# Unit products of a float32 matmul kernel: the low-part products written between the high-part products

## The chip, the cores and the metric

The kernel runs on one core of a Trainium2 chip. The metric is the device time of one execution in microseconds (us). Five engines work side by side, each through its own queue in order: TensorE (PE, its weight loads shown apart as PEld), VectorE (DVE), ScalarE (ACT), GpSimd (POOL) and SyncE (SP), which issues most of the transfers.

## What is computed

One block of a hybrid encoder trunk on 256 tokens of width 2048, all in float32. The parts of the reference that matter here:

```
u = RMSNorm_pre(x)                                # x: 256 x 2048
proj = u @ w_in                                   # q/k/v of two attentions, RWKV inputs, gates
y_a, y_b = stick_breaking(...), forgetting(...)   # 4 heads x 128 each
y_c = rwkv7_time_mix(...)                         # 16 heads x 64, chunks of 64
m = g_a*(y_a @ w_branch_a) + g_b*(y_b @ w_branch_b) + g_c*(y_c @ w_branch_c)
x = x + RMSNorm_post(m @ w_out)
hdn = square(relu(RMSNorm_pre2(x) @ w_mlp_up))    # 2048 -> 8192
x = x + RMSNorm_post2(hdn @ w_mlp_down)           # 8192 -> 2048
```

## The kernel before, in words

Every large product is made in three parts. An operand is split into a high part (rounded by ScalarE to the format `float32r` that TensorE takes) and a low part (what VectorE finds left over): `wsplit` (lines 150 to 160) does so for each weight tile of 128 x 1024 that SyncE brings in (`wraw`, line 145), in line 158 on ScalarE (`whi`) and line 159 on VectorE (`wlo`). Then high times high, high times low and low times high are summed; low times low is left out.

An activation tile `pk` is 128 x 512: 256 columns of the high part and beside them 256 of the low part. So a product of a high weight block with the whole `pk` gives two of the three sums at once, over 512 columns (called a high product here); a product of the low weight block with the first half of `pk` gives the third, over 256 columns (a low product). A weight block of 128 x 128 is loaded into TensorE for each product.

There are two forms of large product. In `tok` (lines 195 to 232; its products stand in lines 204 and 220) the activations are the loaded side and the weights the moving one, so all its products have 512 columns; it makes values, gates, branches and output projections. In `gemm` (line 170) the weights are the loaded side. `gemm` takes one half of a unit: 8 weight blocks (`hi`, `lo`) against 8 activation tiles. `unit` (line 184) calls it twice for one output tile of 128 features, the second time with `last` set. It serves 40 units of the projection (queries, keys, the low-rank inputs, the RWKV inputs). The up-projection of the MLP (`up`, line 1342) calls `gemm` itself for 62 more output tiles, in two halves that stand apart in a list of work with the products of the down-projection (lines 1478 to 1480, all of 512 columns) in between. That makes 204 calls with 16 products each: 1632 high ones (lines 174 and 182) and 1632 low ones (line 178).

Before the change, `gemm` writes all high products first (line 174), then all low ones (line 178). In the second half of a unit the last high product is kept back and closes the sum, behind the low ones (line 182).

TensorE's order is the order in which the program is written, up to the end of the first stage; the other engines' queues are ordered by the framework's scheduler. The attentions and the RWKV recurrence ("mixers") run as threads beside the units: `tick` moves a clock of the program forward by the estimated time of the products just written (`US` = 0.227 us for 512 columns), and a thread whose due time has come writes its next step at that place, so its small products stand inside a unit. A thread says with `yield 3.0` how long its next step has to wait. `gemm` ticks after every second high product and after every fourth low one: 12 `US` in a first half, 10 in a second one. `up` calls `gemm` without a clock.

`sb_mix` (line 428 on) is one such thread. Its chain runs ScalarE (lines 437, 443, 445), VectorE (441, 442, 452, 453), eight masking products on GpSimd (line 456), ScalarE again (line 462, the split) and VectorE (line 463). ScalarE's queue also holds `whi` (line 158) for the units, so what waits there holds up the weights.

Weight tiles of the split kind have three buffers each (`whi`, `wlo`); the split of the next half is written before the products of the present one.

Of the kernel before, what the change touches and what calls it, by code (L numbers as in the profile page):

```python
# [22 lines left out]
US = 0.227  # L23
# [27 lines left out]
def hybrid_block(ctx, tc, xt, x, gains, params, consts, lora, gup, wst, out):  # L51
    nc = tc.nc
    V, A, G, PE = nc.vector, nc.scalar, nc.gpsimd, nc.tensor
# [52 lines left out]
    def step(th):  # L106

        if th["need"] is not None:
            if th["need"] not in at or clock[0] < at[th["need"]] + SETTLE:
                return False  # L110
            th["need"] = None
        if clock[0] < th["due"]:
            return False
        try:
            r = next(th["gen"])
        except StopIteration:
            threads.remove(th)
            return True
        if isinstance(r, str):
            th["need"] = r  # L120
        else:
            th["due"] = clock[0] + r
        return True

    def tick(us):

        clock[0] += us
        while any([step(th) for th in list(threads)]):
            pass
# [40 lines left out]
    def gemm(ps, hi, lo, pks, first, last, tick=lambda us: None):  # L170

        n = len(pks)
        for i in range(n - 1 if last else n):
            PE.matmul(ps, hi[:, i * 128:i * 128 + 128], pks[i], start=first and i == 0, stop=False)  # L174
            if i % 2:
                tick(2 * US)
        for i in range(n):
            PE.matmul(ps[:, 0:T], lo[:, i * 128:i * 128 + 128], pks[i][:, 0:T], start=False, stop=False)  # L178
            if i % 4 == 3:
                tick(2 * US)  # L180
        if last:
            PE.matmul(ps, hi[:, (n - 1) * 128:n * 128], pks[n - 1], start=False, stop=True)  # L182

    def unit(pks):

        ps = gps()
        for h in range(2):
            hi, lo = wnext()
            gemm(ps, hi, lo, pks[8 * h:8 * h + 8], h == 0, h == 1, tick)
        return ps  # L190
# [221 lines left out]
    for h in range(8):  # L412
        ps = qb[h] if h < 3 else unit(upk)
# [641 lines left out]
    for s in ("q", "k"):  # L1055
        lst = []
        for h in range(4):
            ps = unit(upk)
# [12 lines left out]
    for hf in range(2):  # L1071
        for s, mo in (("k", MU_K), ("r", MU_R), ("v", MU_V)):
            for p in range(4 * hf, 4 * hf + 4):
                ps = unit(upk)
# [278 lines left out]
    def up(j):  # L1353
# [3 lines left out]
        def run(hl, half):  # L1357
            if half == 0:
                ps[0] = gps()
            gemm(ps[0], hl[0], hl[1], upk2[8 * half:8 * half + 8], half == 0, half == 1)  # L1360
            if half:
                urgent.append(post)
# [163 lines left out]
    for j in range(2):  # L1526
        up(j)
        ps, post = heads[j]
# [23 lines left out]
    for b in range(4):  # L1552
        for sb in range(2):
            for d, F in enumerate(down(b, sb)):
# [3 lines left out]
                last = b == 3 and sb == 1 and d == SIZES[3] // 4 - 1  # L1558
# [211 lines left out]
```

## Time and profile before

| | |
|---|---|
| runs of the kernel before | 1493.69, 1495.75, 1497.37 us (median 1495.75) |
| span of the profiled execution | 1493.8 us; the page gives no other time for it |
| DVE busy in the span | 1213.1 us (81%) |
| ACT busy in the span | 933.9 us (63%) |
| moved by DMA | 317.70 MB, mean 213 GB/s |

The page of the profile lists the busy time of each engine, the span in 40 slices, the chain of work that ended last, and groups of instructions by line. A row of a group reads: line, engine, operation, output<-inputs, shapes, count | busy time, mean time of one in ns | idle time of the engine before them and who ended it. A row of the timeline reads: start in us, length in us, engine, line, operation, tiles, shapes, count of equal instructions in a row, and in brackets the engine's idle time before it. Products of TensorE overlap, so the length of one is longer than its share of the time: what a product costs is read from the distance between starts.

### The profile page before, as it was taken

How to read it: one execution, taken by the hardware profiler on the slowest of the kernel's cores; microseconds unless marked ns; L12 is line 12 of the kernel's file. 1: busy time of each engine (PE TensorE's matmuls, PEld its weight loads, DVE VectorE, ACT ScalarE, POOL GpSimd, SP SyncE). 2: the span in 40 equal slices, each digit the busy share in tenths (PEclk: the TensorE clock that was granted, in tenths of full speed). 3: DMA queues.
4: the chain of work that ended last, by engine and by line, in shares of the span. 5: the costliest groups of instructions: out<-in, count | busy, mean ns of one | idle time of the engine just before them, and what ended most of it. 6: DMA issues, size and time to landing. Idle time of an engine off the chain costs nothing.

```text
span 1493.8 us, 22852 instructions
## 1 busy us (share of the span) xinstructions
PE 1480.8 (99%) x8427; PEld 1250.7 (84%) x8427; DVE 1213.1 (81%) x1688; ACT 933.9 (63%) x1396; POOL 91.3 (6%) x160
## 2 busy tenths in 40 slices
PE   9999999999999999999999999999999999999997
PEld 8888888888778888788888888888888888888885
DVE  7666677999679798567547788999899999999996
ACT  7465666664576554474444777776766776777663
POOL 0021000100001100000000000000000000000000
PEclk9999999999999999999999999999999999999999
DMA  7545455545544545445755868888888788889874
GB/s 282 188 148 191 163 170 180 172 162 198 171 153 161 184 169 209 144 151 194 269 196 204 275 213 249 255 257 259 242 232 264 238 262 248 260 248 283 259 250 151
DMA packets 107759, 317.70 MB, mean 213 GB/s; under 512 B 10752, under 2 KB 14976, under 8 KB 107392
## 3 DMA queue, kind: packets, MB, share of 16 engines
q1 hardware_dynamic: 94688, 284.39, 54.9%
q0 software_dynamic: 8064, 29.36, 10.5%
q10 hardware_dynamic: 4896, 2.49, 0.6%
q8 instruction: 66, 1.08, 0.3%
q14 instruction: 45, 0.37, 0.1%
HBM read 282.65 MB, written 4.19 MB: 192 GB/s over the span
## 4 chain that ended last, share of the span: by engine, by line
PE 96%; DVE 1%; ACT 1%; issue 1%; POOL 0%; POOLq 0%; DVEq 0%; ACTq 0%
PE gps L220 28%; PE gps L174 23%; PE gps L178 13%; PE gps L204 7%; PE mps L1478 3%; PE mps L1479 3%; PE mps L1480 3%; PE gps L1480 3%; PE gps L1478 2%; PE gps L1479 2%; PE gps L182 2%; PE gps L340 1%; PE mps L791 1%; PE mps L281 0%; PE gps L1237 0%
## 5 line engine op out<-in xcount | busy, mean ns | idle before, releaser
L159 DVE TENSOR_TENSOR wlo<-raw,whi 128x1024 fp32r<-128x1024 f32 x497 | 602.7, 1220 | 157.2 <-ACT whi L158 140.7
L158 ACT ACTIVATE whi<-raw 128x1024 fp32r<-128x1024 f32 x497 | 522.0, 1056 | 249.7 <-PE gps L220 101.1
L174 PE MATMUL gps<-pk,whi 128*128 128x512 f32 x1336 | 336.5, 391 | 0.4 <-ACT whi L158 0.4
L174 PEld LDWEIGHTS gps<-pk,whi 128*128 128x128 f32 x1336 | 247.3, 188 | 48.8 <-ACT whi L158 0.6
L220 PE MATMUL gps<-whi,pk 128*128 128x512 f32 x1136 | 286.0, 391 | 0.0
L220 PEld LDWEIGHTS gps<-whi,pk 128*128 128x128 f32 x1136 | 211.5, 188 | 44.0
L178 PEld LDWEIGHTS gps<-pk,wlo 128*128 128x128 f32 x1424 | 194.1, 190 | 14.1 <-DVE wlo L159 0.3
L178 PE MATMUL gps<-pk,wlo 128*128 128x256 f32 x1424 | 199.3, 282 | 0.0
L220 PE MATMUL gps<-wlo,pk 128*128 128x512 f32 x568 | 155.3, 392 | 0.0
L220 PEld LDWEIGHTS gps<-wlo,pk 128*128 128x128 f32 x568 | 105.7, 188 | 21.9
L1341 DVE TENSOR_TENSOR sp<-raw,sp 128x1024 fp32r<-128x1024 f32 x67 | 81.7, 1220 | 6.7 <-ACT sp L1340 6.5
L1340 ACT ACTIVATE sp<-raw 128x1024 fp32r<-128x1024 f32 x67 | 70.6, 1054 | 19.6 <-DMA raw<-in_wst_dram 6.3
L1369 ACT ACTIVATE sp<-gps 128x512 f32<-128x512 f32 x52 | 31.1, 598 | 72.1 <-PE gps L182 72.1
L204 PE MATMUL gps<-whi,pk 128*128 128x512 f32 x256 | 68.9, 390 | 0.0
L1478 PE MATMUL mps<-whi,fm 128*128 128x512 f32 x168 | 66.1, 394 | 0.0
L1479 PE MATMUL mps<-whi,fm 128*128 128x512 f32 x168 | 65.8, 392 | 0.0
L1480 PE MATMUL mps<-wlo,fm 128*128 128x512 f32 x168 | 65.5, 390 | 0.0
L1440 POOL DMA_DIRECT2D raw<-raw x40 | 34.9, 873 | 431.1 <-DVE raw L1437 111.7
L204 PEld LDWEIGHTS gps<-whi,pk 128*128 128x128 f32 x256 | 47.8, 188 | 9.9
L1480 PE MATMUL gps<-wlo,fm 128*128 128x512 f32 x126 | 49.4, 392 | 0.5 <-DVE wlo L159 0.4
L1478 PE MATMUL gps<-whi,fm 128*128 128x512 f32 x126 | 49.2, 391 | 0.0
L1437 DVE TENSOR_TENSOR raw<-raw,raw 128x1024 f32<-128x1024 f32 x40 | 48.8, 1220 | 0.4
(393 smaller groups left out, 2009.1 us busy)
## 6 DMA issues: line engine op xcount, KB each, us to landing
raw<-in_wst_dram SPq DMA_DIRECT2D x499, 512.0 KB, 4.4
raw<-raw POOLq DMA_DIRECT2D x40, 512.0 KB, 7.6
sp<-in_wst_dram SPq DMA_DIRECT2D x16, 512.0 KB, 5.4
raw<-sp POOLq DMA_DIRECT2D x8, 512.0 KB, 6.9
sp<-raw POOLq DMA_DIRECT2D x8, 512.0 KB, 7.0
x<-in_x_dram SPq DMA_DIRECT2D x8, 256.0 KB, 5.5
xs<-x SPq DMA_DIRECT2D x2, 1024.0 KB, 4.9
x<-xs SPq DMA_DIRECT2D x4, 512.0 KB, 6.2
```

What stands on the lines that cost most here:

```text
L158: A.activation(hi, raw, AF.Copy)
L159: V.tensor_tensor(lo, raw, hi.bitcast(F32), ALU.subtract)
L174: PE.matmul(ps, hi[:, i * 128:i * 128 + 128], pks[i], start=first and i == 0, stop=False)
L178: PE.matmul(ps[:, 0:T], lo[:, i * 128:i * 128 + 128], pks[i][:, 0:T], start=False, stop=False)
L204: PE.matmul(ps[tt], pks[k][:, c:c + 128], w[:, (k - k0) * 512:(k - k0) * 512 + 512], start=k == 0 and part == 0 and w is hl[0], stop=w is ...
L220: PE.matmul(ps[tt], pks[k][:, c:c + 128], w[:, (k - k0) * 512:(k - k0) * 512 + 512], start=k == 0 and part == 0 and w is hl[0], stop=False)
L1340: A.activation(hi, raw, AF.Copy)
L1341: V.tensor_tensor(lo, raw, hi.bitcast(F32), ALU.subtract)
L1437: V.tensor_tensor(x, x, z, ALU.add)
L1478: PE.matmul(Q[f], p, w, start=d == 0 and i == 0, stop=False)
L1479: PE.matmul(Q[f], pl, w, start=False, stop=False)
L1480: PE.matmul(Q[f], p, wl, start=False, stop=d == nd - 1 and i == 1)
```

## The change

Only `gemm` is changed. It writes three high products, then a low and a high one in turn until the high ones are used up, then the low ones that are left. In a second half the closing high product is still the last, and one more low product comes ahead of it. The clock is moved by the whole time of the products: 12 `US` in a first half as before, and 12 instead of 10 in a second half.

```diff
-        for i in range(n - 1 if last else n):
-            PE.matmul(ps, hi[:, i * 128:i * 128 + 128], pks[i], start=first and i == 0, stop=False)
-            if i % 2:
-                tick(2 * US)
-        for i in range(n):
+        lag = 3
+        end = n - 1 if last else n
+
+        def high(i):
+            PE.matmul(ps, hi[:, i * 128:i * 128 + 128], pks[i], start=first and i == 0, stop=last and i == n - 1)
+
+        def low(i):
             PE.matmul(ps[:, 0:T], lo[:, i * 128:i * 128 + 128], pks[i][:, 0:T], start=False, stop=False)
-            if i % 4 == 3:
-                tick(2 * US)
+
+        for i in range(lag):
+            high(i)
+        tick(lag * US)
+        for i in range(n - (1 if last else 0)):
+            low(i)
+            if i + lag < end:
+                high(i + lag)
+                tick(1.5 * US)
+            else:
+                tick(0.5 * US)
         if last:
-            PE.matmul(ps, hi[:, (n - 1) * 128:n * 128], pks[n - 1], start=False, stop=True)
+            low(n - 1)
+            high(n - 1)
+            tick(1.5 * US)
```

In the changed kernel the high products stand in line 177, the low ones in line 180, and every later line is 13 further down (158 and 159 stay; 437 becomes 450, 445 becomes 458, 456 becomes 469, 462 becomes 475).

TensorE's queue, second half of the unit `gps_964` in the first stage (`pk` are the activation tiles, `whi` and `wlo` the weight parts). Before:

```order
L174 MATMUL gps_964<-pk_222,whi_967 128x512
L174 MATMUL gps_964<-pk_225,whi_967 128x512
L174 MATMUL gps_964<-pk_228,whi_967 128x512
L174 MATMUL gps_964<-pk_231,whi_967 128x512
L174 MATMUL gps_964<-pk_244,whi_967 128x512
L174 MATMUL gps_964<-pk_247,whi_967 128x512
L174 MATMUL gps_964<-pk_250,whi_967 128x512
L178 MATMUL gps_964<-pk_222,wlo_968 128x256
L178 MATMUL gps_964<-pk_225,wlo_968 128x256
L178 MATMUL gps_964<-pk_228,wlo_968 128x256
```

The same half now:

```order
L177 MATMUL gps_970<-pk_222,whi_973 128x512
L177 MATMUL gps_970<-pk_225,whi_973 128x512
L177 MATMUL gps_970<-pk_228,whi_973 128x512
L180 MATMUL gps_970<-pk_222,wlo_974 128x256
L177 MATMUL gps_970<-pk_231,whi_973 128x512
L180 MATMUL gps_970<-pk_225,wlo_974 128x256
L177 MATMUL gps_970<-pk_244,whi_973 128x512
L180 MATMUL gps_970<-pk_228,wlo_974 128x256
L177 MATMUL gps_970<-pk_247,whi_973 128x512
L180 MATMUL gps_970<-pk_231,wlo_974 128x256
L177 MATMUL gps_970<-pk_250,whi_973 128x512
L180 MATMUL gps_970<-pk_244,wlo_974 128x256
```

The first low product, which reads the VectorE tile `wlo`, moves from behind seven high products to behind three; four low products in a row remain at the end, of which the last is cut off here.

ScalarE's queue while `sb_mix` runs beside the units (`sbt` and `sbh` are tiles of that thread, `zp` and `zz` of the low-rank inputs, `raw` a weight tile as it came). Before:

```order
L443 ACTIVATE sbt<-sbt 128x768 x2
L593 ACTIVATE tmp_842<-gps_774 36x256
L158 ACTIVATE whi_876<-raw_874 128x1024
L445 ACT_TABLE_LOAD
L445 ACTIVATE sbt<-sbt 128x1536
L596 ACTIVATE zp_844<-tmp_843,par 36x256
L158 ACTIVATE whi_907<-raw_905 128x1024
L610 ACT_TABLE_LOAD
L610 ACTIVATE zz<-zz 32x256
L233 ACTIVATE tmp_900<-gps_851 128x256
L158 ACTIVATE whi_939<-raw_937 128x1024
L462 ACTIVATE sbh<-sbt 128x768
```

The same stretch now:

```order
L456 ACTIVATE sbt<-sbt 128x768
L606 ACTIVATE tmp_842<-gps_774 36x256
L158 ACTIVATE whi_879<-raw_877 128x1024
L456 ACTIVATE sbt<-sbt 128x768
L609 ACTIVATE zp_844<-tmp_843,par 36x256
L458 ACT_TABLE_LOAD
L458 ACTIVATE sbt<-sbt 128x1536
L158 ACTIVATE whi_917<-raw_915 128x1024
L623 ACT_TABLE_LOAD
L623 ACTIVATE zz<-zz 32x256
L246 ACTIVATE tmp_910<-gps_851 128x256
L158 ACTIVATE whi_939<-raw_937 128x1024
```

One of the two exponentials (line 443, now 456) and the scaling of the low-rank input (line 596, now 609) have moved to between the weight split and the table load ahead of the logarithm (line 445, now 458).

VectorE's queue for the same chain, where the two operations that follow the logarithm stand (lines 452 and 453, now 465 and 466). Before:

```order
L452 TENSOR_TENSOR sbt<-sbm,sbt 128x768
L597 SCALAR_TENSOR_TENSOR zz<-tmp_843,omu,zp_844 36x256
L453 TENSOR_TENSOR sbt<-sbt 128x768
L159 TENSOR_TENSOR wlo_908<-raw_905,whi_907 128x1024
L452 TENSOR_TENSOR sbt<-sbm,sbt 128x768
```

Now:

```order
L610 SCALAR_TENSOR_TENSOR zz<-tmp_843,omu,zp_844 36x256
L465 TENSOR_TENSOR sbt<-sbm,sbt 128x768 x2
L466 TENSOR_TENSOR sbt<-sbt 128x768
L159 TENSOR_TENSOR wlo_918<-raw_915,whi_917 128x1024
L247 TENSOR_TENSOR g_146_909<-gps_851,tmp_910 128x256
```

Both halves of the first operation now stand ahead of the first half of the second, which GpSimd waits for.

## Prediction, made before the changed kernel was run

> **What bounds the kernel now.** I read the page first: engines, slices, waits of TensorE.
>
> ```profile
> span 1493.8 us, 22852 instructions
> ...
> PE 1480.8 (99%) x8427; PEld 1250.7 (84%) x8427; DVE 1213.1 (81%) x1688; ACT 933.9 (63%) x1396; POOL 91.3 (6%) x160
> ...
> L178 PE MATMUL gps<-pk,wlo 128*128 128x256 f32 x1424 | 199.3, 282 | 0.0
> ```
>
> ```profile
> PE gps L174 <- ACT whi L158: 0.4, 1, 0.4
> ```
>
> TensorE is busy for 1480.8 of 1493.8 us, and the second row, from the list of its waits, is the only wait of line 174: 0.4 us in one place. So the time is set by the pace at which TensorE takes products, and by no other engine. The change adds and removes no product; it can only alter that pace, or bring new waits.
>
> The pace is the distance between starts. The chain that ended last has a long run of nothing but high products (`tok`), and the timeline of TensorE has one unit alone:
>
> ```profile
> 54.28 19.06 PE gps L220 x84
> ```
>
> ```profile
> 24.57 2.00 PE L174 MATMUL gps<-pk,whi 128*128 128x512 f32 x8
> 26.41 1.12 PE L178 MATMUL gps<-pk,wlo 128*128 128x256 f32 x8
> 27.36 1.78 PE L174 MATMUL gps<-pk,whi 128*128 128x512 f32 x7
> 28.98 1.11 PE L178 MATMUL gps<-pk,wlo 128*128 128x256 f32 x8
> 29.93 0.40 PE L182 MATMUL gps<-pk,whi 128*128 128x512 f32 x1
> 30.16 2.00 PE L174 MATMUL gps<-pk,whi 128*128 128x512 f32 x8
> ```
>
> A settled high product costs 19.06/84 = 0.227 us. The unit from 24.57 to 30.16 costs 5.59 us for 16 pairs of a high and a low product: 0.3494 a pair. Its first eight low ones take 27.36 - 26.41 = 0.95, or 0.119 each. But its first eight high ones take 1.84, or 0.230 each: behind low products the high ones are slower than in a long run. A 256-column product at half the price of a 512-column one would cost 0.1135. So there is a reserve: if all went at 0.227 and 0.1135, a pair would cost 0.3405, 0.009 less than now, and 1632 pairs 14.5 us less. The question is how much of it the new order can reach.
>
> **The pace of products in turn.** No stretch of this trace alternates as the new order does, but there are places with one high product between low ones, and a few that show the extremes (timeline of TensorE; the first rows are small products of the mixers with the same shapes):
>
> ```profile
> 116.78 0.28 PE L472 MATMUL mps<-sbh,tri 128*128 128x256 f32 x1
> 116.90 0.28 PE L472 MATMUL mps<-sbl,tri 128*128 128x256 f32 x1
> 117.01 0.39 PE L479 MATMUL mps<-sbh,tri 128*128 128x512 f32 x1
> 117.24 0.40 PE L481 MATMUL mps<-sbl,tri 128*128 128x256 f32 x2
> 117.47 1.08 PE L174 MATMUL gps<-pk,whi 128*128 128x512 f32 x4
> ...
> 457.64 0.39 PE L220 MATMUL gps<-wlo,pk 128*128 128x512 f32 x1
> 457.87 0.28 PE L1004 MATMUL mps<-syh,gup 128*128 128x256 f32 x1
> 457.98 0.28 PE L1004 MATMUL mps<-syl,gup 128*128 128x256 f32 x1
> 458.10 0.28 PE L1004 MATMUL mps<-syh,gup 128*128 128x256 f32 x1
> 458.22 0.27 PE L1004 MATMUL mps<-z,gup 128*128 128x256 f32 x1
> ...
> 825.89 0.40 PE L1237 MATMUL gps<-pk,w 128*128 128x512 f32 x1
> 826.13 0.39 PE L1237 MATMUL gps<-pk,whi 128*128 128x512 f32 x1
> ```
>
> A low product right behind a high one costs 0.11 (457.87 to 457.98), a later one of the run 0.12 (457.98 to 458.22, two of them). A single high product between low ones costs 0.23 in both places (117.01 to 117.24, 457.64 to 457.87), and the two low ones behind the first of them 0.115 each. The dearest high product, the second behind a run of low ones, costs 0.24 (825.89 to 826.13).
>
> How I read it: settled runs cost 0.227 and 0.120, together 0.347 a pair, so a unit would cost 16 x 0.347 = 5.55 without any switching. It costs 5.59: switching from one size to the other costs 0.04 a unit on balance (the first low product gains, the next few high ones lose). The new order still ends each half with three low products (four in a second half), so I keep that loss. Of a first half, five pairs stand in turn (three high ones ahead, five times low-high, three low ones left); of a second half four, and its closing high one. With 102 units that is 102 x 9 = 918 pairs. For them I take the nearest rows, 0.23 + 0.115 = 0.345 against the settled 0.347: 918 x (-0.002) = -1.8 us. The bounds: 0.23 + 0.11 = 0.34 gives -6.4; 0.24 + 0.12 = 0.36 gives +11.9; with 0.23 + 0.12 = 0.35 it is +2.8. I keep -6.4 and +11.9 for the cases below.
>
> The weight loads speak on the low side of that question:
>
> ```profile
> 26.19 1.13 PEld L178 LDWEIGHTS gps<-pk,wlo 128*128 128x128 f32 x8
> ```
>
> The load for the first low product starts at 26.19, 0.22 before that product (26.41): as soon as the last high product starts, and not earlier. So one load can run ahead, no more, and behind a low product the next load has only 0.11 to 0.12 us of cover, in either order. In the Trainium skill, TensorE: Matmul & The Clock Gate, section "LDWEIGHTS (loading the stationary operand)", a load costs its columns divided by 1.2 GHz; for 128 columns that is an estimate of 0.107 us. By that rule the loads fit beneath even a low product at 0.1135, a run of low products is not held by them, and there is nothing for the change to hide: the term would be 0 in place of -1.8. The trace neither shows the load's own pace in these runs nor contradicts the rule, since its load records (0.19 each) overlap.
>
> **The waits that move.** The low weights are now wanted after three high products instead of eight (or seven): 3 x 0.23 = 0.69 us behind the start of the half, 1.15 (0.92) earlier. In the trace almost all low parts are ready long before. The tight place is the unit that runs beside the masking of `sb_mix` (timeline, the engines ACT, POOL, DVE and PE):
>
> ```profile
> 87.13 1.49 ACT L445 ACTIVATE sbt<-sbt 128x1536 f32<-128x1536 f32 x1
> 88.52 0.50 ACT L596 ACTIVATE zp<-tmp,par 36x256 f32<-36x256 f32 x1
> ...
> 96.74 0.85 ACT L462 ACTIVATE sbh<-sbt 128x768 fp32r<-128x768 f32 x1 [3.83 <-POOL sbt L456]
> 97.49 1.04 ACT L158 ACTIVATE whi<-raw 128x1024 fp32r<-128x1024 f32 x1
> ```
>
> ```profile
> 90.95 7.43 POOL L456 TENSOR_TENSOR sbt<-sbt,con 128x128 f32<-128x128 f32 x8 [0.79 <-DVE sbt L453]
> ```
>
> ```profile
> 91.93 0.94 DVE L452 TENSOR_TENSOR sbt<-sbm,sbt 128x768 f32<-128x768 f32 x1
> ...
> 98.56 1.23 DVE L159 TENSOR_TENSOR wlo<-raw,whi 128x1024 fp32r<-128x1024 f32 x1 [3.02 <-ACT whi L158]
> ...
> 102.11 2.35 DVE L159 TENSOR_TENSOR wlo<-raw,whi 128x1024 fp32r<-128x1024 f32 x2
> ```
>
> ```profile
> 98.58 1.88 PE L174 MATMUL gps<-pk,whi 128*128 128x512 f32 x7 [0.38 <-ACT whi L158]
> 100.30 1.12 PE L178 MATMUL gps<-pk,wlo 128*128 128x256 f32 x8
> ...
> 101.49 2.00 PE L174 MATMUL gps<-pk,whi 128*128 128x512 f32 x8
> ```
>
> ScalarE stands 3.83 us at line 462 for GpSimd, and the split of the weights is queued behind it; it ends at 98.53 and TensorE starts at 98.58, having waited 0.38. With the order of before alone, the low parts would come at 98.56 + 1.23 = 99.79 against a need at 98.58 + 0.69 = 99.27 (0.52 short), and the next at about 102.11 + 1.2 = 103.3 against 101.49 + 0.52 + 0.69 = 102.70 (0.6 short): 1.1 us. That is the lower bound of this term.
>
> The queues change too. On ScalarE the second exponential (0.85 in the trace, like line 462's row of the same shape) and line 596 (0.50) move ahead of the logarithm of line 445, so it ends about 1.3 later than 87.13 + 1.49 = 88.62, at 89.9; the weight split that stood there is ahead of it in both. On VectorE both halves of line 452 (0.94 each) now stand ahead of line 453: GpSimd starts about 1.3 + 0.94 - 0.4 (line 597 is out of the way) = 1.85 later, at 92.8. Line 462 then starts at 96.74 + 1.85 = 98.6, the weights are split at 98.6 + 0.85 + 1.04 = 100.4, and TensorE waits 1.9 more than before at the high products. Its low part comes 1.23 later, 101.65, against 100.45 + 0.69 = 101.14: 0.5 more. The next low part follows 3.55 behind (103.34 - 99.79), at 105.2; TensorE, with five high and eight low products left at 101.65, starts the next half at 103.75 and wants it at 104.45: 0.75 more. Sum 1.9 + 0.5 + 0.75 = 3.1 us. I take 3.1, with 1.1 and 3.6 as bounds (3.6 if the second masking half, queued behind two low parts on VectorE, starts 0.5 later still).
>
> A second kind of short place lies in the MLP, where VectorE is nearly full:
>
> ```profile
> 880.00:1436.00 556.00, 555.51 (x2833) 473.53 (x2832) 513.67 (x598) 391.43 (x522) 47.78 (x55) 1.00 0.85 252
> ```
>
> ```profile
> 1177.32 1.22 DVE L159 TENSOR_TENSOR wlo<-raw,whi 128x1024 fp32r<-128x1024 f32 x1
> ```
>
> ```profile
> 1177.72 1.75 PE L174 MATMUL gps<-pk,whi 128*128 128x512 f32 x7
> ```
>
> VectorE is busy 513.67 of 556 us there, 92%. This low part ends at 1178.54; the products begin at 1177.72 and would want it at 1178.41, 0.13 short. For all such places I allow 0.5 us (an estimate, about four of them), between 0 and 1.
>
> Free of cost: a high buffer is held until 0.35 before the end of a first half instead of 0.95. Three buffers cover it; the split that waits for it has the whole half in between (2.8 us) for 1.04 + 1.23 us of work. Without that cover it would cost up to 0.6 a half. The clock of the program now runs 24 `US` a unit, not 22, so the mixers' steps stand up to two units earlier and their pauses are some 8% shorter in real time. They have the same work, and TensorE waits for them nowhere by more than 0.4 us now; what that moves is in the walk above.
>
> **The sum.** -1.8 + 3.1 + 0.5 = +1.8 us on the span of 1493.8, so 1495.6. The three timed runs lie between 1493.69 and 1497.37, so the profiled execution is at the fast end, 1.95 below the median 1495.75. Against that median the forecast is 1497.5. A measurement of this kernel can tell about 0.3%, 4.5 us, from no change; so this is no change.
>
> **The rivals.** *Faster: the two sizes lock together.* If each low product in turn cost what the first of a run costs (0.11), each high one 0.23 or less, and the switching loss at the end of a half went too (102 x 0.04 = 4.1 us), the pace would gain 6.4 + 4.1 = 10.5; with 3.6 of waits the sum is -6.9: 1489. For it: the first low product really is cheaper. Against it: the high product behind a low one is at 0.23 to 0.24 in every row above, not at 0.227, and halves still end on three or four low ones.
>
> *Slower: the high products never settle.* Behind a low run the high ones need several to get back to 0.227 (eight of them average 0.230 at 24.57). In turn none gets the time. If they stay between 0.23 and 0.24 while the low ones stay at 0.12, a pair costs 0.355: 918 x 0.008 = +7.3, with waits +10.9: 1506.5. It decides from about 0.348 a pair on, where the sum passes +4.5. For it: the second high product at 0.24; against it: both single high products at 0.23 and low ones at 0.115 behind them.
>
> *Slower: VectorE in the MLP.* 124 halves there want their low part about 1 us earlier. If one in ten were 0.35 short, that is 12 x 0.35 = 4.3 us on top: 1502. Against it: 8% of VectorE's time is free, and each wait of TensorE gives the following low parts more time.
>
> **How the numbers follow.** Forecast (within 0.3%, 1491.3 to 1500.2): 0.49. Locked pace, 1489: 0.19. Unsettled pace, 1506.5: 0.20; VectorE, 1502: 0.12. So faster 0.19, same 0.49, slower 0.32. The range reaches from the locked case, 1489, to just under the unsettled one, 1505.5; the dearest pace, +11.9, lies outside.
>
> **What would show it.** In the profile of the changed kernel: starts in a half of a unit, pair by pair, at 0.345 on average between the third high product and the last low ones (0.34 or 0.355 would be the rivals); line 177 waiting for line 158 some 2 us near 98, line 180 waiting for line 159 there by about 1.2; waits of line 180 for line 159 in the MLP of under 1 us in total. I am wrong if the pairs in turn lie outside 0.340 to 0.350, or if waits of TensorE add up to over 6 us.

## The result and the profile after

| | before | changed |
|---|---|---|
| median of the timed runs | 1495.02 us (1493.69 to 1497.37, 5 runs) | 1502.95 us (1502.66 to 1503.37, 5 runs) |
| ratio to before, 95% interval | | 1.0054 (1.0044 to 1.0065) |
| span of the profiled execution | 1493.8 us | 1501.1 us (its time 1502.92 us) |

The changed kernel is slower by 7.9 us, 0.54%. The forecast was 1497.5 us and "no change": the time lies within the range that was given, but outside the 0.3% and 5.5 us above the forecast. The spans differ by 7.3 us, and that is the difference to be explained here.

The page of the changed kernel, its span, its engines, and the two groups of unit products:

```profile
span 1501.1 us, 22857 instructions
...
PE 1485.1 (99%) x8427; PEld 1249.4 (83%) x8427; DVE 1217.6 (81%) x1688; ACT 936.3 (62%) x1396; POOL 94.9 (6%) x160
...
L177 PE MATMUL gps<-pk,whi 128*128 128x512 f32 x1424 | 462.3, 395 | 0.5 <-DVE junk L1498 0.3
L180 PE MATMUL gps<-pk,wlo 128*128 128x256 f32 x1424 | 329.6, 282 | 1.3 <-DVE wlo L159 1.1
```

TensorE is still 99% busy. The busy time of line 180 looks as if it had jumped (329.6 us, where the same products had 199.3 in line 178), but that is only how overlapping records are added up: a low product that stands alone shows 0.28 us, eight in a row show 1.12 us together. Busy time can't be compared between two orders; distances between starts can. The waits of TensorE, longest first (engine and line that waits, what for: sum in us, times, longest):

```profile
PE gps L233 <- DVE wlo L159: 1.2, 1, 1.2
...
PE gps L180 <- DVE wlo L159: 1.1, 3, 0.5
PE mps L934 <- DVE XT L925: 0.6, 2, 0.3
...
PE gps L177 <- ACT whi L158: 0.2, 1, 0.2
```

The new waits named here come to 2.3 us (lines 233 and 180). Much of the rest of the 7.3 us is pace, and it shows in one half of a unit in the MLP. Before, eight high and eight low products, and the next product behind them:

```profile
1100.43 1.98 PE L174 MATMUL gps<-pk,whi 128*128 128x512 f32 x8
1102.25 1.11 PE L178 MATMUL gps<-pk,wlo 128*128 128x256 f32 x8
1103.20 0.40 PE L1478 MATMUL mps<-whi,fm 128*128 128x512 f32 x1
```

A half with the same number of products in the changed kernel:

```profile
1101.55 0.84 PE L177 MATMUL gps<-pk,whi 128*128 128x512 f32 x3
1102.23 0.28 PE L180 MATMUL gps<-pk,wlo 128*128 128x256 f32 x1
1102.34 0.39 PE L177 MATMUL gps<-pk,whi 128*128 128x512 f32 x1
1102.58 0.28 PE L180 MATMUL gps<-pk,wlo 128*128 128x256 f32 x1
1102.69 0.40 PE L177 MATMUL gps<-pk,whi 128*128 128x512 f32 x1
1102.93 0.28 PE L180 MATMUL gps<-pk,wlo 128*128 128x256 f32 x1
1103.05 0.40 PE L177 MATMUL gps<-pk,whi 128*128 128x512 f32 x1
1103.29 0.28 PE L180 MATMUL gps<-pk,wlo 128*128 128x256 f32 x1
1103.40 0.40 PE L177 MATMUL gps<-pk,whi 128*128 128x512 f32 x1
1103.64 0.65 PE L180 MATMUL gps<-pk,wlo 128*128 128x256 f32 x4
1104.12 0.40 PE L177 MATMUL gps<-pk,whi 128*128 128x512 f32 x1
1104.35 0.40 PE L1491 MATMUL mps<-whi,fm 128*128 128x512 f32 x1
```

Before: 1103.20 - 1100.43 = 2.77 us. Now: 1104.35 - 1101.55 = 2.80. The four pairs in turn from 1102.23 to 1103.64 take 1.41 us, 0.3525 each, where the forecast had 0.345.

Over all unit products, from the starts in the trace (which holds them to the nanosecond), waits and other long gaps left out: a high product went from 0.2287 to 0.2327 us, a low one from 0.1190 to 0.1176, a pair from 0.3477 to 0.3503. That is 2.6 ns for each of 1632 pairs, **4.2 us**. The 887 pairs in turn that no other product interrupts average 0.3519 us (low 0.1169, high 0.2350).

Where the rest is, stage by stage (bounds in the time of before, distances from the starts of TensorE's products in the two traces):

| stage, us | changed - before, us | what it is |
|---|---|---|
| 0 to 330, projection | +2.27 | pace, and 2.75 us more in long gaps between unit products; 1.0 us less in other products |
| 330 to 690, mixers and `tok`, no unit in it | +2.88 | no product of a unit; see e2 and the queue of VectorE below |
| 690 to 881 | +0.23 | pace |
| 881 to 1440, MLP | +1.89 | unit products +3.52, down-projection -1.63 |
| to the end | +0.02 | |

The down-projection's -1.63 us is most likely nothing that the change did: run e11 below, of the kernel before once more, has -1.52 there, too.

### The profile page after: what moved, and what is told of

It reads as the page before. It is cut to its first block, busy times and chain, and to the rows that moved or that the text cites. A ratio compares the mean times of both kernels' runs of the same rounds, so it can differ in the third digit from the quotient of the medians.

```text
span 1501.1 us, 22857 instructions
## 1 busy us (share of the span) xinstructions
PE 1485.1 (99%) x8427; PEld 1249.4 (83%) x8427; DVE 1217.6 (81%) x1688; ACT 936.3 (62%) x1396; POOL 94.9 (6%) x160
## 4 chain that ended last, share of the span: by engine, by line
PE 93%; DVE 3%; ACT 2%; issue 1%; POOL 0%; DMA 0%; POOLq 0%; DVEq 0%; SPq 0%; ACTq 0%
PE gps L233 27%; PE gps L177 23%; PE gps L180 12%; PE gps L217 7%; PE mps L1492 3%; PE mps L1493 3%; PE mps L1491 3%; PE gps L1491 2%; PE gps L1492 2%; PE gps L1493 2%; DVE wlo L159 1%; PE gps L353 1%; PE mps L804 1%; ACT whi L158 1%; PE gps L1250 0%
## 5 line engine op out<-in xcount | busy, mean ns | idle before, releaser
L177 PE MATMUL gps<-pk,whi 128*128 128x512 f32 x1424 | 462.3, 395 | 0.5 <-DVE junk L1498 0.3
L180 PE MATMUL gps<-pk,wlo 128*128 128x256 f32 x1424 | 329.6, 282 | 1.3 <-DVE wlo L159 1.1
L177 PEld LDWEIGHTS gps<-pk,whi 128*128 128x128 f32 x1424 | 261.0, 188 | 51.6 <-ACT pk L1392 0.7
L180 PEld LDWEIGHTS gps<-pk,wlo 128*128 128x128 f32 x1424 | 250.1, 189 | 18.7 <-DVE wlo L159 3.5
L177 PE MATMUL gps<-pk,sp 128*128 128x512 f32 x208 | 68.3, 395 | 0.0
```

## The experiments

The change has two parts, the order of the products and the places and sum of the clock's ticks; and it stands in two places, `unit` and `up`. The theories before the runs: that a pair in turn is dearer (the pace), that TensorE waits for low parts that are now wanted earlier, and that the clock moves the mixers' steps to worse places. Runs with an interval had 5 to 11 timed runs each; "before" is the kernel before on the same chip (1495.61 us for e1 to e4, 1495.21 for e5 to e8, a single run of 1495.66 for e9 to e11).

### e1: the new order, the clock as before

```diff
+        marks = {2: 2, 4: 2, 6: 2, 11: 2, 15: 2} if last else {2: 2, 4: 2, 6: 2, 8: 2, 12: 2, 16: 2}
+        lag = 3
+        steps = [(high, i) for i in range(lag)]
+        for i in range(n):
+            steps.append((low, i))
+            if i + lag < end:
+                steps.append((high, i + lag))
...
+        for k, (op, i) in enumerate(steps):
+            op(i)
+            if k + 1 in marks:
+                tick(marks[k + 1] * US)
```

`marks` are the places and amounts of the clock, counted in products as the kernel before has them.

> The new order of products, but the program's clock moved as before (the same amounts after the same number of products: 12 US in a first half, 10 in a second). Theory 1 (two causes): the change lost about 7.3 us on the profiled span, about 3.5 of it by the pace of products in turn (0.351 us a pair against 0.347 settled) and the rest by the clock, which lets the mixers' steps stand earlier. Then this kernel is about 3.5 us slower than before (ratio 1.0023), and the stage from 330 to 690 us, which has no unit in it, is as long as before (within 0.5 us; the changed kernel lost 2.9 there). Theory 2 (order alone): the low parts are wanted earlier and everything follows from that; then this kernel is as slow as the changed one, 7 to 8 us over before.

1501.06 us, ratio 1.0037 (1.0024 to 1.0049). Span +4.1: 54 to 330 us +2.3, 330 to 690 +0.3, MLP +1.7. Pairs in turn 0.3518. So the order alone loses, and it leaves the middle of the kernel alone. In the MLP it loses by pace. In the projection only 0.9 of the 2.3 us are pace by the mean pair; the rest are longer gaps between unit products, two of them waits for low parts (0.7 us in the list of waits).

### e2: the old order, the clock of the change

The products stand as before, and `marks` repeats the new clock by the count of products.

```diff
+        marks = {3: 3, 5: 1.5, 7: 1.5, 9: 1.5, 11: 1.5, 12: 0.5, 13: 0.5, 14: 0.5, 16: 1.5} if last else {
+            3: 3, 5: 1.5, 7: 1.5, 9: 1.5, 11: 1.5, 13: 1.5, 14: 0.5, 15: 0.5, 16: 0.5}
+        steps = [(high, i) for i in range(end)] + [(low, i) for i in range(n)]
```

> The old order of products, but the clock moved as in the change (the same amounts after the same number of products, 12 US in either half). Theory 1: about 3.5 to 4 us slower than before (ratio 1.0025), with 2 to 3 us of it between 330 and 690 us. Theory 2: no slower than before (within 0.5 us).

1500.56 us, ratio 1.0036 (1.0023 to 1.0049). The mean products are those of before (0.2287 and 0.1190), so nothing of this is pace. The first two waits of TensorE:

```profile
PE gps L177 <- ACT whi L158: 2.9, 2, 1.5
PE gps L227 <- DVE wlo L159: 1.2, 1, 1.2
```

The first is two waits for the high weights in the projection, 1.45 us at 102.19 us beside `sb_mix` and 1.49 at 196.03; the second stands in the middle of the kernel. Between 330 and 690 us the run loses 2.95 us, as the changed kernel does (2.88), while e1 has 0.3 there. So this part of the loss belongs to the clock. The two parts alone, added up (4.1 + 4.6 in spans) are more than the change (7.3): in the changed kernel the 2.9 us for high weights are 0.2.

### e3 and e4: the whole change in one place

`gemm_turn` is the changed `gemm`, and `gemm` is the old one. e3 calls `gemm_turn` in `up` only, e4 in `unit` only. The edit of e3, against the kernel before:

```diff
-            gemm(ps[0], hl[0], hl[1], upk2[8 * half:8 * half + 8], half == 0, half == 1)
+            gemm_turn(ps[0], hl[0], hl[1], upk2[8 * half:8 * half + 8], half == 0, half == 1)
```

> The new order in the MLP's up-projection alone (124 of 204 calls, no clock there), everything else as before. Theory 1: only the pace counts, 124/204 of about 3.5 us: 2.1 us slower than before (ratio 1.0014), no wait of TensorE for a low part above 0.5 us. Theory 2: waits for low parts in the MLP, where VectorE is 92% busy; then there are some us of them and they show in the list of waits.

> The whole change, with its clock, in the units of the projection alone (80 of 204 calls); the up-projection as before. Theory 1: 1.4 us of pace and 3.5 to 4 us of the clock: 5 to 5.5 us slower than before (ratio 1.0035). Theory 2: what e3 does not show is here too, so that both add to the 7.3 us of the change; it puts the loss between 54 and 330 us, where the units are, and not behind them.

e3: 1498.64 us, ratio 1.0020 (1.0012 to 1.0029). e4: 1500.96, 1.0036 (1.0024 to 1.0048). The two excesses add up to 0.56%, the change has 0.54%. `up` has no clock, so e3 is pace or waits; its waits for low parts in the MLP come to 0.8 us (one wait of 1.0 us there, for the tile `junk` of VectorE's line 1512, is none for a low part), its unit products there take 4.0 us more than before, and its pairs in turn 0.3520 us. So this is pace for the most part, about 0.2% for 62 of the 102 units. The theory that low parts come late falls for the MLP as the main cause. In e4 pace is the small part: 0.6 us by the mean pair of the projection's units. Its span is 6.1 us longer, 2.7 of it between 54 and 330 us, nearly all in longer gaps between unit products, and 3.4 between 330 and 690, where no unit stands.

### e5 and e6: more switching, and less

e5 has one high product ahead in place of three, so that nearly all pairs stand in turn. e6 goes in turn by twos. Against e1:

```diff
-        lag = 3
+        lag = 1
```

```diff
+        for i in range(0, n, 2):
+            steps += [(low, i), (low, i + 1)] + [(high, k) for k in (i + 3, i + 4) if k < end]
```

Both have the clock of before, like e1.

> The clock as before and the new order with one high product ahead instead of three, so that 13 pairs of a unit stand in turn, not 9. Theory A (a high product right behind a low one never settles, and costs the same 4 ns a pair over the settled 0.347 us wherever it stands): pairs in turn at 0.351 us again; 1326 of them cost 1326 x 0.004 = 5.3 us, 1.6 more than with three ahead, so 5.5 to 6 us over before by the profile, and waits for low parts on top (they are wanted after 0.23 us). Theory B (the price comes from two products that read the same activation tile at a certain distance): with another distance the pair costs something else, by 2 ns or more.

> The clock as before, three high products ahead, then two low and two high ones in turn: half as many changes of size. Theory A (price by the change of size): the pace loses half of what it lost with one and one, about 1.8 us, so 2 to 2.5 us over before. Theory C (the loss comes from the low products being wanted early or from where the runs end, not from changes of size): as slow as one and one, 4 us over before.

e5: 1505.71 us, ratio 1.0066 (1.0054 to 1.0078). e6: 1499.23, 1.0025 (1.0016 to 1.0035). The mean pair, with the number of places in TensorE's order where another product follows a low one:

| kernel | such places | mean pair, us |
|---|---|---|
| before | 207 | 0.3477 |
| e6 | 721 | 0.3490 |
| changed | 1124 | 0.3503 |
| e5 | 1530 | 0.3516 |

Times 1632 pairs, each such place costs 4.1 to 4.8 ns over the kernel before: (0.3490 - 0.3477) x 1632 = 2.1 us over 514 places, 4.2 over 917, 6.3 over 1323. So over the whole kernel the pace loss goes with the number of switches. It is no fixed price of one switch, though, but a mean over two places: with one low product at a time, a switch costs 6.2 to 6.6 ns in the units of the MLP and 1.6 to 2.6 in those of the projection (e1, e3, e4, e5 and the change); with two (e6) it costs 3.8 and 4.7. That the three quotients above agree is in part chance.

In e5 a pair in turn costs 0.352 us again, so theory B, a price set by the distance between two products that read the same activation tile, is not borne out. e5 also shows what the pairs do when there are many in a row (TensorE's timeline in the MLP):

```profile
1102.41 0.28 PE L179 MATMUL gps<-pk,wlo 128*128 128x256 f32 x1
...
1102.75 0.28 PE L179 MATMUL gps<-pk,wlo 128*128 128x256 f32 x1
...
1103.11 0.28 PE L179 MATMUL gps<-pk,wlo 128*128 128x256 f32 x1
...
1103.47 0.28 PE L179 MATMUL gps<-pk,wlo 128*128 128x256 f32 x1
...
1103.81 0.28 PE L179 MATMUL gps<-pk,wlo 128*128 128x256 f32 x1
...
1104.17 0.28 PE L179 MATMUL gps<-pk,wlo 128*128 128x256 f32 x1
...
1104.53 0.40 PE L179 MATMUL gps<-pk,wlo 128*128 128x256 f32 x2
```

The distances are 0.34, 0.36, 0.36, 0.34, 0.36, 0.36: one cheap pair and two dear ones, over and over. In the MLP of the changed kernel the same holds by position in a half, from the starts of 477 pairs: first pair 0.347, second 0.358, third 0.356, fourth 0.346, fifth 0.358. Only the first pair behind settled products, and each third one after it, has the price that the prediction took. In the projection the cycle is much weaker.

### e7 and e8: more on the clock at the end of a second half

Both have the old order and the old places of the clock; e7 adds 2 `US` behind the last product of a second half (24 a unit, the sum of the change, and one place more), e8 adds 1 to the last place that is there (23 a unit). The amounts of a second half before, in e7 and in e8:

```diff
-        marks = {2: 2, 4: 2, 6: 2, 11: 2, 15: 2}
+        marks = {2: 2, 4: 2, 6: 2, 11: 2, 15: 2, 16: 2}
+        marks = {2: 2, 4: 2, 6: 2, 11: 2, 15: 3}
```

> The old order and the old places of the clock's steps, with 2 US added at the end of a second half, so that either half moves the clock by 12 US. If the sum counts (24 US a unit instead of 22): as slow as with the whole new clock, 4 to 5 us over before, 2 to 3 of it between 330 and 690 us. If only the places of the steps inside a half count: within 1 us of before.

> The old order with 23 US a unit, half of what the change adds to the clock (one US more at the last step of a second half). If the loss grows with the clock: 2 to 2.5 us over before. If it hangs on how single steps of two mixers fall beside each other: anything between -1 and +5 us, and not at the same places.

e7: 1497.07 us, ratio 1.0006 (0.9998 to 1.0015), no difference that shows in the time. e8: 1501.47, 1.0039 (1.0027 to 1.0051). So the theory that the loss grows with the sum of the clock falls: the whole step costs at most 0.15%, half of it 0.39%. The traces say the same of the stage from 330 to 690 us: e7 is 1.8 us longer there, e8 4.0, the change 2.9. So e7 is not free in that stage; its span comes out level because its MLP is 1.65 us shorter, 1.42 of that in the down-projection, as in e11 below. What counts seems to be where the steps of the mixers happen to land. e8's first two waits are of the same kind as those of e2:

```profile
PE gps L176 <- ACT whi L158: 1.6, 2, 1.3
PE gps L226 <- DVE wlo L159: 1.5, 1, 1.5
```

A slower clock was not tried.

### e9 and e10: another size of the low product

In the order and clock of e1 the low product takes 384 columns, or 128, in place of 256. e9 thus adds low times low for 128 columns, and e10 leaves half of the low sums out.

```diff
-            PE.matmul(ps[:, 0:T], lo[:, i * 128:i * 128 + 128], pks[i][:, 0:T], start=False, stop=False)
+            PE.matmul(ps[:, 0:384], lo[:, i * 128:i * 128 + 128], pks[i][:, 0:384], start=False, stop=False)
```

e10 has 128 in place of 384. The question was why a pair in turn is dear. The cover theory (A1): behind a short low product the next weight load has too little time, so 384 columns bring the high product back to 0.227 us. Its rival (A2): the change of size itself costs.

> As the order alone (three high products ahead, clock as before), but each low product of a half runs over 384 columns instead of 256: it adds the low weight times half of the low activation, a part of the sum that the kernel leaves out. Not to be faster, but for the price of the high product behind a low one. Theory A1 (cover: the weight load of the high product starts when the low product starts, and does not quite fit beneath 256 columns): beneath 384 columns, 0.170 us, it fits, so the high product in turn is back at 0.227 and the pair at 0.397 to 0.40. Theory A2 (the change of size itself unsettles TensorE): the high product stays at 0.232 to 0.236 and the pair at 0.404 or more.

> As the order alone, but each low product of a half runs over 128 columns only: it leaves out the low weight times the second half of the tokens. Theory A1 (cover): the load sets the distance from a low to the next high product, which stays at 0.107 to 0.117 us though the product is half as long, and the high product is as dear as before or dearer (0.235 or more). Theory A2 (change of size): the low product costs clearly less than 0.1 us, the high one 0.235 or more.

A single run of each: 1590.97 us and 1502.08 us; only the pairs are of use. In e9 they take 0.407 us (low 0.174, high 0.233; 906 pairs). The high product does not come back to 0.227 although the load has half as much cover again, which speaks against A1 as the whole cause and for A2. In e10 they take 0.3425 us (low 0.060, high 0.282; 901 pairs); TensorE's products and then its weight loads in the first unit:

```profile
25.38 0.22 PE L179 MATMUL gps<-pk,wlo 128*128 128x128 f32 x1
25.44 0.45 PE L176 MATMUL gps<-pk,whi 128*128 128x512 f32 x1
25.72 0.22 PE L179 MATMUL gps<-pk,wlo 128*128 128x128 f32 x1
```

```profile
25.38 0.19 PEld L176 LDWEIGHTS gps<-pk,whi 128*128 128x128 f32 x1
25.49 0.19 PEld L179 LDWEIGHTS gps<-pk,wlo 128*128 128x128 f32 x1
25.72 0.19 PEld L176 LDWEIGHTS gps<-pk,whi 128*128 128x128 f32 x1
```

The low product starts 0.06 ahead of the high one, but the next load starts 0.11 behind the load before it and not 0.06, and the pair ends at 0.34 = 0.11 + 0.23. The runs of low products at the end of a half of e10 say the same: 306 of them stand 0.111 apart, though one behind a high product takes 0.060. So here a load of 0.11 us sets the pace in place of a product of 0.06, and half as many columns brought the pair only from 0.352 to 0.3425. This is cover, but it is the case of 128 columns; with 256 the product (0.113 to 0.12) is about as long as the load. In the Trainium skill, TensorE: Matmul & The Clock Gate, section "LDWEIGHTS (loading the stationary operand)", a load is its columns divided by 1.2 GHz, by estimate 0.107 us for 128; the trace agrees with its 0.11. But the conclusion that the prediction drew from the rule, that a low product of 256 columns hides the load and the order makes no difference, does not give the 4.2 us that were measured.

Why two pairs of three are dear with 256 columns, and why the high product stays at 0.233 behind 384, is left open.

### e11: the kernel before once more

> The order and the clock of before, written as a list of steps: the same instructions as before on every engine. A second profile of the same program, to see how far two profiled executions differ in a stage. Either theory: the span within 2 us of 1493.8, the stages up to 880 us within 0.5 us; the MLP stage, where transfers and VectorE are fullest, may differ by 1 to 2 us.

A single run: 1493.75 us, span 1491.9. Each stage up to 881 us lies within 0.25 us of the other trace of the same program, the MLP 1.67 us below it, 1.52 of that in the down-projection. So differences of a few tenths ahead of 881 us can be read from single traces, and in the MLP a difference under 2 us can't. The MLP's loss is read from its unit products (+3.52) and from e3's interval.

## Why the prediction held in its range and failed in its pace

The time lies in the stated range (1489 to 1505.5), but outside the 0.3% that the prediction itself called no change, and one of its own signs of being wrong came up: the pairs in turn lie at 0.352, outside 0.340 to 0.350. That the range held is due to its width, which reached almost to the slow rival, and in part to luck: the sum at the end of this section has 8.9 us of underrated loss (pace and clock) against 3.4 us the other way, of which 1.6 is scatter. And the prediction took the profiled execution of before for a fast one, since its span lies 1.95 us below the median. It was not: a time lies about 1.8 us above its own span in these runs (1495.60 for the span of 1493.8, 1502.92 for 1501.1). The time of the slow rival, 1495.75 + 10.9, should read 1506.7 in place of 1506.5; nothing hangs on it.

**The pace, the step that failed.** The prediction took "the nearest rows, 0.23 + 0.115 = 0.345", for all 918 pairs, and got -1.8 us. It was 0.352, and +4.2 us. Its own bounds (0.34 to 0.36) held it, and what happened is what its slow rival said, "the high products never settle" (0.355 a pair, +7.3): high 0.235, in the middle of the 0.23 to 0.24 that the rival gave, and low 0.117 for its 0.12. The rows that it used were each a high product that stood alone among other products, with no pair ahead of it. They are a first pair, and in the MLP, in the changed kernel and in e5, first pairs do cost 0.347. The price of a pattern that repeats can't be had from a single instance of it. The row that pointed the right way was the second high product behind a low run, at 0.24, and it was put down as the dearest case.

**The place that loses most of it.** The prediction saw no difference between the units of the projection and those of the MLP. In the projection the old order was itself unsettled (0.3494 a pair in the quoted unit), and in that stage the pace cost only 0.5 us (3.3 of unit products less 2.75 of long gaps). In the MLP the high products of before follow the down-projection's, which also have 512 columns, and cost 0.227 from the first one on, so that there was nothing to gain there: 3.5 of the loss lies in its unit products.

**The waits.** 3.1 us beside `sb_mix` and 0.5 in the MLP were forecast. All long gaps in the projection grew by 2.75 us and those in the MLP by under 0.1, so the sum is near, but the walk was right only in part. The timeline of the changed kernel at that place:

```profile
87.69 1.49 ACT L458 ACTIVATE sbt<-sbt 128x1536 f32<-128x1536 f32 x1
...
91.98 6.27 POOL L469 TENSOR_TENSOR sbt<-sbt,con 128x128 f32<-128x128 f32 x8 [4.93 <-DVE sbt L466]
...
96.60 0.85 ACT L475 ACTIVATE sbh<-sbt 128x768 fp32r<-128x768 f32 x1 [3.53 <-POOL sbt L469]
...
98.44 0.96 PE L177 MATMUL gps<-pk,whi 128*128 128x512 f32 x3 [0.18 <-ACT whi L158]
...
99.70 0.39 PE L180 MATMUL gps<-pk,wlo 128*128 128x256 f32 x1 [0.30 <-DVE wlo L159]
...
101.70 1.09 PE L177 MATMUL gps<-pk,whi 128*128 128x512 f32 x4
103.24 0.39 PE L180 MATMUL gps<-pk,wlo 128*128 128x256 f32 x1 [0.46 <-DVE wlo L159]
```

The two low parts are late as the prediction had it for the queues of before (0.52 and 0.6): after three high products the first was due at 98.44 + 0.69 = 99.13 and came at 99.70, the second, behind one closing and three high products, was due at 101.70 + 0.92 = 102.62 and came at 103.24, 0.57 and 0.62 late. e1, which has the new order and the old clock, has the same two waits (at 99.47 and 103.01 us). What failed is the 2 us that the changed queues were to add.

Line 458 starts at 87.69 and not 1.3 later than before (87.13), since the chain ahead of it ran earlier (the weight split ahead of it at 84.19 in place of 84.77). GpSimd starts at 91.98 (forecast 92.8), and ScalarE needs only 4.62 us after that to go on (96.60 - 91.98), where it needed 5.79 before (96.74 - 90.95). So line 475 is not late at all, and TensorE waits 0.18 us for the high weights, not 1.9 more than before. The long gaps between 92 and 103 us grew by about 1 us; the others lie near 239 and 257 us, which the prediction did not look at. GpSimd's masking spans 6.27 us for 7.43; why was not tried. That the place can go the other way is shown by e2, which waits 1.45 us there with the same clock.

**The clock, "free of cost".** This failed too, for 2.9 us between 330 and 690 us, where no unit stands and the clock's new reading alone has moved the mixers (e2 has it, e1 has not). The one wait that the trace names there, VectorE's queue first, then TensorE's, in the changed kernel:

```profile
457.97 0.91 DVE L784 TENSOR_TENSOR At<-g,lw 128x256 f32<-128x256 f32 x1
458.81 0.41 DVE L782 SCALAR_TENSOR_TENSOR At<-kkr,tha 128x256 f32<-128x256 f32 x1
459.14 0.41 DVE L1011 TENSOR_TENSOR g<-g,gn 128x256 f32<-128x256 f32 x1
459.48 1.21 DVE L159 TENSOR_TENSOR wlo<-raw,whi 128x1024 fp32r<-128x1024 f32 x1
```

```profile
457.51 2.00 PE L233 MATMUL gps<-whi,pk 128*128 128x512 f32 x8
460.74 1.19 PE L233 MATMUL gps<-wlo,pk 128*128 128x512 f32 x4 [1.23 <-DVE wlo L159]
```

The low part is queued behind steps of the RWKV recurrence (lines 784 and 782) and of its gates (line 1011) that stood elsewhere before, and TensorE stands for 1.23 us. The prediction's reason, that TensorE waits nowhere by more than 0.4 us, said where the queues were full in the old arrangement and nothing of a new one. The other 1.7 us of that stage are spread over small products and short waits (line 934, 0.6 us) and were not pinned down.

The sum: the span was forecast at 1495.6 and came to 1501.1, 5.5 more. Pace +6.0, clock in the middle +2.9, long gaps -0.8, the scatter of the down-projection -1.6, small differences in the projection -1.0.

## What to carry to other kernels

Price an alternating order from a place that alternates for several turns, and if the trace has none, put the forecast nearer to the dear row than to the mean. Products of 512 and 256 columns were cheapest here in long runs of one size, behind products of the same size; each return from the short to the long one cost 4 to 5 ns on average, more where the long run was settled before (6 to 7 ns in the MLP) and less where it was not. Where a clock of the program places the work of other threads, moving its ticks is a change of its own, worth up to 0.4% here with the order of the products as before, and is better tried apart from the order of the products.

## What the runs showed of the hardware

In the MLP of this kernel, pairs of 512 and 256 columns in turn do not settle at one price but go through 0.346, 0.358 and 0.356 us again and again. With 128 columns in the short product they settle at 0.340 (fourth and fifth pair of a half): 0.11 and 0.23 us between the starts of the loads. Two profiled executions of the same program differ by 1.7 us in the MLP and by under 0.25 us in any other stage.
